# Two heads' attention scores on the two 64-row halves of TensorE, in a float32 model of two transformer blocks

## The chip, the cores and the metric

The program runs on one core of a Trainium2 chip. The metric is the device time of one execution in microseconds, the median of several runs. TensorE multiplies matrices; VectorE (DVE), ScalarE (ACT) and GpSimd (POOL) do the work between; SyncE (SP) issues most of the DMA transfers that bring weights from memory.

## What is computed

Two blocks, one behind the other, on 256 tokens of width 1024, in float32. The first has a retention and a convolution branch and a mixture of 32 experts. The second has two layers; each mixes tokens with four groups of four heads (Fourier, neighbourhood attention, spatial gating, differential attention) and has an MLP. Its first layer is also computed for a context of 256 tokens, whose keys and values the tokens attend to as well. The part of the reference that matters:

```python
def neighbourhood_attention(q, k, v, k_ctx, v_ctx, rpb, rows):
    ...
    s_loc = jnp.einsum('brqhd,brikhd->bhrqik', qg, k_band).astype(jnp.float32) * scale + bias.astype(jnp.float32)
    s_loc = jnp.where(in_win[:, None, :], s_loc, -jnp.inf)
    s_loc = s_loc.reshape(bsz, h, rows, GRID_W, wr * GRID_W)
    s_ctx = jnp.einsum('brqhd,blhd->bhrql', qg, k_ctx).astype(jnp.float32) * scale
    p = jax.nn.softmax(jnp.concatenate([s_loc, s_ctx], axis=-1), axis=-1).astype(v.dtype)
    ...
```

Four heads of width 64, 256 queries; 256 own keys (with bias and window) and 256 keys of the context in the layers. On the context side the same routine runs with the context's own 256 keys, without bias.

## The kernel before

One core does everything in order of stages: the first block, the experts, then the two layers of the second block. The context side of the second block runs beside the experts: `moe` (line 1091) calls `side()` after each expert, which takes the next step of `context_side`. What the context side's matmuls write goes to the two PSUM banks of pool `pf`; the experts use the two of `pm`, and `pa` has four.

In front of the experts stands a branch: `overflow` (line 1157) loads the largest number of tokens that any expert got (`maxcnt`) into a register of every engine and runs a slow path if it is over 32, `with tc.If(rv > 32)` (line 1162). It is not over 32 here, but every engine's instructions in front of the branch stay in front of it.

Weights are float32, in tiles of 1 MB that SyncE loads ahead (`half`, line 243). A matmul with weights goes as three products of tiles split in a high and a low part (`split_w`, line 277). All other matmuls, the scores too, are plain float32; the hardware runs each of them as two passes, and the trace has a record for each pass.

Neighbourhood attention, `na` (line 1366), has eight units per call: two chunks of two heads (c), two halves of the queries (qt), two heads in a chunk (hh). The queries of chunk c lie with head 0 on rows 0 to 63 and head 1 on rows 64 to 127, and so do the keys. A matmul contracts over all 128 rows, so `head_pads` (line 1317) makes two tiles of zeros, and `fill_pad` (line 1326) copies each head's rows out of PSUM into the half that is not to be zero, four copies for two chunks. `two_w` (line 1516) is what the projection calls for that. A unit's first step multiplies such padded queries with the keys of the layer (`own`) and of the context (`kvc`), adds the bias by a matmul (`nab`, with the flipping matrix `k`), takes the softmax (minimum on VectorE, exponential on ScalarE into a tile `e`, or `a` on the context side, then a scaling with the reciprocal sum); its second step, `attend` (line 1348), transposes the probabilities and copies them into `pt`, and after the second head `pv` (line 1355) multiplies them with the values, each head on 64 columns of the array.

The order of the layers' mixer is the string `MIX` (line 26); `mixer` (line 1572) takes a letter at a time: digits are projections, n and d first steps of a unit of neighbourhood and differential attention, b the second step of the oldest open unit, p a part of the output projection (`pj`), and so on. Scores take their PSUM bank from `pm` and `pf` in turn there. On top of that a scheduler, which runs when the program is built, moves instructions of an engine past one another by its own estimate of times. `diff` (line 1451) has the differential attention, with scores `ks`,`qs` over 96 rows.

```python
MIX = "012nndtd3nbbbdndbbbvbndfdbnnsbnpbgdbdxbbbbbp"
```

## Time and profile before

| | |
|---|---|
| runs shown, median (lowest to highest) | 1782.87 us (1780.77 to 1783.07) |
| the profiled execution: its own time | 1776.12 us |
| the profiled execution: span of the trace | 1774.3 us |
| TensorE, matmuls | 1657.3 us busy, 93% of the span |
| TensorE, weight loads | 1317.0 us, 74% |
| VectorE, ScalarE, GpSimd | 54%, 41%, 3% |
| memory read | 486.91 MB |
| granted TensorE clock, mean | 0.982 of 2.4 GHz |

The profile is of one execution, whose own time is the second row; the trace runs from its first to its last instruction. Busy time of TensorE is that of its matmul records, which overlap one another: two passes that start 0.12 us apart each last 0.28 us or more. So rates are read from starts, not from durations. In a timeline a row may stand for several records in a row ("x4"), and its duration is then that from the first start to the last end.

### The profile page before, as it was taken

Reading aid. Unit: us, or ns where it says so; the run is one execution under the profiler, and the core shown is the slowest. Engines: PE = TensorE matmul, PEld = TensorE weight load, DVE = VectorE, ACT = ScalarE, POOL = GpSimd, SP = SyncE. Lnnn points to the kernel's source line nnn. Section 1 sums busy time; section 2 is a strip of 40 time slices with the busy share of each in tenths; the row PEclk is TensorE's granted clock in tenths of the full one; section 3 lists DMA queues with packets and bytes.
Section 4 is the critical chain, followed back from the end, with each engine's and each line's share of the span. In section 5 each row is a group of like instructions: output and inputs, shape, how many; then the busy total and the mean of one; then the engine's idle time right before and its main releaser. Section 6 shows DMA issues by size and latency. Waiting matters only on the chain.

```text
span 1774.3 us, 31435 instructions
## 1 busy us (share of the span) xinstructions
PE 1657.3 (93%) x13088; PEld 1317.0 (74%) x13088; DVE 961.2 (54%) x1719; ACT 724.0 (41%) x1257; POOL 61.6 (3%) x104
## 2 busy tenths in 40 slices
PE   4999999999888998999999997999999999899998
PEld 1678766667565556776677666878999998689998
DVE  5626556467223445544454457586545456766555
ACT  2414434343223433333233336565444445645443
POOL 0000000000000000000000001010000000100000
PEclk9899999999899999999999999999999999989999
DMA  9654588977699999989979997725877746245551
GB/s 372 278 211 169 199 317 310 345 278 265 240 420 420 421 395 407 379 365 420 416 318 401 421 394 268 232 81 172 291 253 264 263 165 208 76 130 188 192 190 43
DMA packets 79060, 495.83 MB, mean 279 GB/s; under 512 B 8928, under 2 KB 15744, under 8 KB 22464
## 3 DMA queue, kind: packets, MB, share of 16 engines
q1 hardware_dynamic: 74496, 478.30, 70.6%
q0 software_dynamic: 3152, 10.47, 2.0%
q10 hardware_dynamic: 1264, 4.98, 0.7%
q8 instruction: 105, 1.72, 0.4%
q14 instruction: 43, 0.35, 0.1%
HBM read 486.91 MB, written 6.82 MB: 278 GB/s over the span
## 4 chain that ended last, share of the span: by engine, by line
PE 64%; DVE 3%; DMA 3%; ACT 2%; issue 2%; POOL 0%; DVEq 0%; ACTq 0%; POOLq 0%
PE pf L200 23%; PE pm L200 19%; PE acc L200 11%; PE pa L200 5%; PE pj L200 3%; PE pm L203 1%; DMA w<-in_w_in 1%; PE pf L203 1%; DMA w<-in_e 1%; PE pada L200 1%; DVE wl L209 1%; DMA w<-in_w_out 1%; DVE sm L1337 1%; ACT e L206 0%; ACT wh L206 0%
## 5 line engine op out<-in xcount | busy, mean ns | idle before, releaser
L209 DVE TENSOR_TENSOR wl<-w,wh 128x1024 fp32r<-128x1024 f32 x346 | 422.4, 1225 | 385.4 <-PE pa L200 100.5
L206 ACT ACTIVATE wh<-w 128x1024 fp32r<-128x1024 f32 x346 | 362.8, 1059 | 407.1 <-PE pa L200 169.5
L200 PE MATMUL pf<-hh,wh 128*128 128x256 f32 x592 | 167.0, 284 | 4.6 <-ACT hh L206 2.4
L200 PE MATMUL pf<-hh,wl 128*128 128x256 f32 x592 | 164.4, 283 | 2.1 <-DVE wl L209 2.1
L200 PE MATMUL pf<-hl,wh 128*128 128x256 f32 x592 | 165.3, 281 | 0.5 <-DVE hl L209 0.5
L200 PE MATMUL acc<-hh,wh 128*128 128x256 f32 x512 | 143.5, 280 | 0.0
L200 PE MATMUL acc<-hl,wh 128*128 128x256 f32 x512 | 142.9, 279 | 0.0
L200 PE MATMUL acc<-hh,wl 128*128 128x256 f32 x512 | 142.9, 279 | 0.0
L200 PE MATMUL pm<-w,xg 128*32 128x256 f32 x2048 | 131.2, 387 | 2.7 <-ACT sm L206 1.8
L200 PEld LDWEIGHTS pf<-hh,wh 128*128 128x128 f32 x592 | 111.8, 189 | 9.8 <-ACT hh L206 3.1
L200 PEld LDWEIGHTS pf<-hh,wl 128*128 128x128 f32 x592 | 110.5, 189 | 5.0 <-DVE wl L209 2.8
L200 PEld LDWEIGHTS pf<-hl,wh 128*128 128x128 f32 x592 | 111.8, 189 | 1.5 <-DVE hl L209 0.9
L200 PEld LDWEIGHTS pm<-w,xg 128*32 128x32 f32 x2048 | 66.6, 111 | 50.9 <-issue 11.2
L200 PEld LDWEIGHTS acc<-hh,wh 128*128 128x128 f32 x512 | 96.4, 188 | 5.9 <-ACT wh L206 4.2
L200 PEld LDWEIGHTS acc<-hh,wl 128*128 128x128 f32 x512 | 96.8, 189 | 0.0
L200 PEld LDWEIGHTS acc<-hl,wh 128*128 128x128 f32 x512 | 96.4, 188 | 0.0
L200 PE MATMUL pada<-w,csil 128*32 128x512 f32 x576 | 83.7, 613 | 5.6 <-DMA w<-in_ada_w 5.6
L200 PE MATMUL pm<-w,ex 128*32 128x256 f32 x1024 | 63.6, 388 | 24.0 <-issue 22.3
L200 PE MATMUL pm<-hh,wh 128*128 128x256 f32 x256 | 71.7, 280 | 0.0
L200 PE MATMUL pm<-hl,wh 128*128 128x256 f32 x256 | 71.7, 280 | 0.0
L200 PE MATMUL pm<-hh,wl 128*128 128x256 f32 x256 | 71.5, 279 | 0.0
L200 PEld LDWEIGHTS pm<-w,ex 128*32 128x32 f32 x1024 | 33.8, 111 | 46.6 <-issue 28.9
(512 smaller groups left out, 3484.7 us busy)
## 6 DMA issues: line engine op xcount, KB each, us to landing
w<-in_e SPq DMA_DIRECT2D x192, 1024.0 KB, 12.1
w<-in_ff SPq DMA_DIRECT2D x96, 1024.0 KB, 5.6
w<-in_ada_w SPq DMA_DIRECT2D x72, 1024.0 KB, 7.1
w<-in_w_in SPq DMA_DIRECT2D x54, 1024.0 KB, 7.8
w<-in_w_out SPq DMA_DIRECT2D x16, 1024.0 KB, 7.0
w<-in_ret_w_o SPq DMA_DIRECT2D x4, 1024.0 KB, 5.2
w<-in_w_su SPq DMA_DIRECT2D x3, 1024.0 KB, 6.5
adab<-in_ada_b SPq DMA_DIRECT2D x9, 256.0 KB, 12.6
```

Of the source, the lines that this page charges most:

```text
L200: return self.nc.tensor.matmul(out, lhsT, rhs, start=start, stop=stop, skip_group_check=True)
L203: return self.nc.tensor.transpose(out, in_, self.ident)
L206: return self.nc.scalar.activation(out, in_, f, **k)
L209: return self.nc.vector.tensor_tensor(out, a, b, op=op)
L1337: self.nc.vector.tensor_reduce(mn, s, AX.X, ALU.min)
```

## The change

`na` no longer takes padded queries but the queries as they come out of the projection, scaled by -0.125 in the one copy out of PSUM (`two_w` with a pair). A new inner function `scores` computes both heads of a chunk for one half of the queries: it takes two PSUM banks, and for each kind of keys multiplies rows 0 to 63 of the queries and keys into the first bank and rows 64 to 127 into the second; then bias and softmax of both. It runs in the first step of head 0; the first step of head 1 does nothing any more. `head_pads` remains for the context's differential attention.

```diff
-    def head_pads(self, w):
+    def head_pads(self):
 
         pads = []
         for c in range(2):
-            t = self.t4([P, 4, 256], F32, "pad") if w == 32 else self.t2([P, 2, 256], F32, "pad")
+            t = self.t4([P, 4, 256], F32, "pad")
...
-    def na(self, pads, ks, vs, bias, put):
+    def na(self, qs, ks, vs, bias, put):
...
         n = 2 * len(ks)
-        pts = {}
+        pts, es = {}, {}
+
+        def scores(c, qt):
+            ps = [self.ps() for _ in range(2)]
+            for (i, k), hh in itertools.product(enumerate(ks), range(2)):
+                r = slice(64 * hh, 64 * hh + 64)
+                self.mm(ps[hh][:, i * 256:(i + 1) * 256], qs[r, c, qt * P:(qt + 1) * P], k[r, c, :], i == 0, True)
+            for hh, p in enumerate(ps):
+                if bias is not None:
+                    self.mm(p[:, :256], self.flip, bias[:, qt, :, 2 * c + hh, :], False, True)
+                sm = self.sm([P, 1])
+                es[c, qt, hh] = e = self.softmax_parts(p[:, :n * P], n * P, sm)
+                self.nc.vector.reciprocal(sm, sm)
+                self.scaled(e, sm, n * P, POOL[0])
 
         def unit(c, qt, hh):
-            h = 2 * c + hh
-            p = self.ps()
-            for i, k in enumerate(ks):
-                self.mm(p[:, i * 256:(i + 1) * 256], pads[c][:, hh, qt * P:(qt + 1) * P], k[:, c, :], i == 0, True)
-            if bias is not None:
-                self.mm(p[:, :256], self.flip, bias[:, qt, :, h, :], False, True)
-            sm = self.sm([P, 1])
-            e = self.softmax_parts(p[:, :n * P], n * P, sm)
-            self.nc.vector.reciprocal(sm, sm)
-            self.scaled(e, sm, n * P, POOL[0])
+            if hh == 0:
+                scores(c, qt)
             yield
             if hh == 0:
                 pts[c, qt] = self.t4([P, 2, 4, P], F32, "pt")
-            self.attend(e, pts[c, qt][:, hh], n)
+            self.attend(es[c, qt, hh], pts[c, qt][:, hh], n)
...
+            elif isinstance(d, tuple):
+                self.act(d[0], p, scale=d[1])
...
-        npad = self.head_pads(64)
-        self.lin(self.chunk(W[0]), 8, 512, [WJob(lhs, self.two_w(npad, nk))])
+        nq = new("nq")
+        self.lin(self.chunk(W[0]), 8, 512, [WJob(lhs, self.two_w((nq, -0.125), nk))])
...
-        na = self.na(npad, [nk, kvc[0]], [nv, kvc[1]], bias, put)
+        na = self.na(nq, [nk, kvc[0]], [nv, kvc[1]], bias, put)
```

`mixer` makes and fills `nq` in the same way.

The order of TensorE's instructions moves with it. First the branch in front of the experts, before (`wh`, `wl`, `hh`, `hl` are the context's value projection, `cnt` counts tokens):

```order
L200 MATMUL pf_3409<-wh_3458,hh_2818 128x512
L200 MATMUL pf_3409<-wl_3459,hh_2818 128x512
L200 MATMUL pf_3409<-wh_3458,hl_2819 128x512
L200 MATMUL pf_4030<-kvc_2793,pad_3277 128x256
L1161 TENSOR_LOAD maxcnt
L1162 COMPARE_AND_BRANCH
```

One score of the context stands in front of the branch, nothing else of its attention. Now:

```order
L200 MATMUL pm_3240<-cnt,router 128x32 x2
L200 MATMUL pm_3240<-cnt,sm_3238 128x32 x3
L200 MATMUL pf_4024<-kvc_2793,nq_3277 128x256
L200 MATMUL pf_4025<-kvc_2793,nq_3277 128x256
L203 MATMUL pf_4043<-ident_81,a_741_4029 128x128 x2
L203 MATMUL pf_4047<-ident_81,a_744_4036 128x128 x2
L200 MATMUL pf_4051<-pt_4042,kvc_2793 64x128
L1161 TENSOR_LOAD maxcnt
L1162 COMPARE_AND_BRANCH
```

Two scores, four transposes of two heads' probabilities and one product with the values stand in front of it, and the five count matmuls, which stood ten matmuls ahead of the projection's end, stand behind the projection.

Second, the first scores of the first layer's mixer, before (`pf` and `pm` are the two banks):

```order
L200 MATMUL pf_10831<-own_10458,pad_10465 128x256
L200 MATMUL pf_10831<-kvc_10398,pad_10465 128x256
L200 MATMUL pf_10831<-nab_10459,k_1942_10395 128x256
L200 MATMUL pm_10842<-own_10458,pad_10465 128x256
L200 MATMUL pm_10842<-kvc_10398,pad_10465 128x256
L200 MATMUL pm_10842<-nab_10459,k_1942_10395 128x256
```

Head 0 and its bias, then head 1 and its bias. Now:

```order
L200 MATMUL pf_10819<-own_10452,nq_10459 128x256
L200 MATMUL pm_10820<-own_10452,nq_10459 128x256
L200 MATMUL pf_10819<-kvc_10392,nq_10459 128x256
L200 MATMUL pm_10820<-kvc_10392,nq_10459 128x256
L200 MATMUL pf_10819<-nab_10453,k_1941_10389 128x256
L200 MATMUL pm_10820<-nab_10453,k_1941_10389 128x256
```

The two heads alternate, and the two biases follow. The second layer's first scores stand alike; the second scores of the first layer stand head by head, four in a row, with both biases behind.

Third, the first layer's third scores, before (head 0 alone; head 1 follows 39 rows later):

```order
L203 MATMUL pf_11153<-ident_81,e_11062 128x128 x4
L200 MATMUL pf_11170<-own_10458,pad_10467 128x256
L200 MATMUL pf_11170<-kvc_10398,pad_10467 128x256
L200 MATMUL pf_11170<-nab_10459,k_1942_10395 128x256
L203 MATMUL pm_11115<-ident_81,e_11040 128x128 x4
```

All of these are 128 rows on 128 columns. Now:

```order
L203 MATMUL pm_11103<-ident_81,e_11039 128x128 x4
L200 MATMUL pf_11158<-own_10452,nq_10459 128x256
L200 MATMUL pf_11158<-kvc_10392,nq_10459 128x256
L200 MATMUL pf_11158<-nab_10453,k_1941_10389 128x256
L200 MATMUL pm_11147<-pt_11095,own_10452 64x128 x4
L200 MATMUL pm_11147<-pt_11095,kvc_10392 64x128 x4
L200 MATMUL pf_11180<-ks_10735,qs_10734 128x512
L200 MATMUL pm_11159<-own_10452,nq_10459 128x256
L200 MATMUL pm_11159<-kvc_10392,nq_10459 128x256
L200 MATMUL pm_11159<-nab_10453,k_1941_10389 128x256
L200 MATMUL pm_11188<-ks_10735,qs_10734 128x512
```

The two heads stand apart, each between matmuls of other shapes. The fourth scores and those of the second layer from the second on are apart as well; in the fourth, eight products with the values stand even between a head's own keys and the context's.

## Rows read from the trace of the kernel before

**Rows 1.** Busy time by stage: stretch, us, engines' busy us (records), granted clock, DMA share, GB/s.

```profile
545.00:1075.00 530.00, 488.19 (x4744) 350.56 (x4738) 260.24 (x476) 177.10 (x348) 15.81 (x33) 0.99 0.97 396
...
1088.00:1235.00 147.00, 136.56 (x945) 117.99 (x944) 100.06 (x223) 83.24 (x161) 17.18 (x21) 0.98 0.53 160
1441.00:1590.00 149.00, 137.23 (x933) 118.48 (x932) 101.62 (x217) 85.59 (x165) 11.99 (x14) 0.95 0.43 137
```

The engines are PE, PEld, DVE, ACT, POOL.

**Rows 2.** The same view around the branch.

```profile
440.00:450.00 10.00, 8.56 (x42) 6.53 (x40) 4.16 (x21) 2.30 (x8) 0.00 (x0) 1.00 0.54 199
450.00:460.00 10.00, 4.84 (x23) 4.87 (x24) 1.00 (x5) 0.46 (x1) 0.50 (x1) 0.52 0.15 58
```

**Rows 3.** Timeline of PE, first scores: start us, us, engine, line, operation, out<-in, rows*columns, count.

```profile
1132.96 0.59 PE L200 MATMUL pf<-own,pad 128*128 128x256 f32 x2
1133.39 0.59 PE L200 MATMUL pf<-kvc,pad 128*128 128x256 f32 x2
```

**Rows 4.** Timeline of PE in the expert stage: matmuls of 32 columns, and of 32 rows.

```profile
463.38 3.98 PE L200 MATMUL pm<-w,xg 128*32 128x256 f32 x64 [0.61 <-ACT sm L206]
...
494.93 0.29 PE L200 MATMUL acc<-yh,sc 32*128 32x256 f32 x4
495.05 0.28 PE L200 MATMUL acc<-yl,sc 32*128 32x256 f32 x4
```

**Rows 5.** Timeline of PE at changes of shape, in the mixer and in the expert stage.

```profile
1156.62 0.28 PE L200 MATMUL pa<-hh,wl 128*128 128x256 f32 x1
1156.83 0.43 PE L200 MATMUL pm<-pt,own 128*64 128x128 f32 x2
1157.19 0.39 PE L200 MATMUL pa<-hh,wh 128*128 128x256 f32 x1
1157.42 0.28 PE L200 MATMUL pa<-hl,wh 128*128 128x256 f32 x1
1157.54 0.28 PE L200 MATMUL pa<-hh,wl 128*128 128x256 f32 x1
...
490.48 0.70 PE L200 MATMUL pf<-kvc,pad 128*128 128x256 f32 x2
491.11 1.07 PE L200 MATMUL pm<-w,ex 128*32 128x256 f32 x16
```

**Rows 6.** The line of the branch: engine, operation, count, ns min/median/max, first and last start.

```profile
L1162 PEldq COMPARE_BRANCH  x1: 5329/5329/5329, 449.1 to 449.1; - x1
```

**Rows 7.** Timeline of all engines around the branch.

```profile
447.99 0.67 PE L200 MATMUL pf<-kvc,pad 128*128 128x256 f32 x2
...
448.70 0.42 DVE L1337 TENSOR_REDUCE sm<-pf 128x1 f32<-128x256 f32 x1 [0.82 <-PE pf L200]
...
449.16 0.47 ACT L206 ACTIVATE a<-pf,sm 128x256 f32<-128x256 f32 x1 [0.57 <-DVE sm L1337]
449.53 0.19 ACT L206 ACTIVATION_READ_ACCUMULATOR a<-pf,sm 128x1 f32 x1
454.66 0.49 DVE L209 TENSOR_TENSOR oh<-router,pos 128x128 f32<-128x128 f32 x2 [5.41 <-PEq L1162]
455.07 0.16 DVE L1381 RECIPROCAL sm<-sm 128x1 f32<-128x1 f32 x1
...
455.26 0.35 DVE L218 TENSOR_SCALAR a<-a,sm 128x256 f32<-128x256 f32 x1
...
461.95 0.37 ACT L206 ACTIVATE pt<-pf 128x256 f32<-128x256 f32 x1
```

**Rows 8.** Timelines of ACT and PE: the context's queries and keys out of PSUM.

```profile
433.71 1.55 ACT L206 ACTIVATE pad<-pf 64x256 f32<-64x256 f32 x4 [1.56 <-PE pf L200]
435.29 0.60 ACT L206 ACTIVATE kvc<-pf 128x512 f32<-128x512 f32 x1
...
435.31 0.50 PE L200 MATMUL pf<-wh,hh 128*128 128x512 f32 x1 [1.00 <-ACT pad L206]
```

**Rows 9.** Timeline of PE, last third of the first mixer: a wait.

```profile
1187.08 0.66 PE L203 MATMUL pm<-ident,e 128*128 128x128 f32 x4 [1.20 <-ACT pt L206]
```

More of the change, by code (lines that the diff above doesn't have):

```diff
@@ L1554, in context_mixer @@
         yield
-        yield from itertools.islice(self.in_turn(self.na(npad, [nk], [nv], None, put), 0), 1, None, 2)
-        dpad = self.head_pads(32)
+        yield from itertools.islice(self.in_turn(self.na(nq, [nk], [nv], None, put), 0), 1, None, 2)
+        dpad = self.head_pads()
         self.lin(self.chunk(W[1]), 8, 512, [WJob(lhs, self.two_w(dpad, dk))])
@@ L1581, in mixer @@
         bias = self.na_bias(l, held)
-        npad = self.head_pads(64)
+        nq = new("nq")
         dq, fa, sv, su = (None,) * 4
-        na = self.na(npad, [nk, kvc[0]], [nv, kvc[1]], bias, put)
+        na = self.na(nq, [nk, kvc[0]], [nv, kvc[1]], bias, put)
         qk_d = [self.tc.dram_tile([P, 1024], F32, name=f"{n}_d{l}") for n in ("q", "k")]
@@ L1589, in mixer @@
             if step == "0":
-                self.lin(w or self.chunk(W[0]), 8, 512, [WJob(lhs, self.two_w(npad, nk))])
+                self.lin(w or self.chunk(W[0]), 8, 512, [WJob(lhs, self.two_w((nq, -0.125), nk))])
             elif step == "t":
```

## The prediction

> **What bounds the kernel now.** I read the busy time by stage first. The expert stage waits for weights: from 545 to 1075 us the DMA engines are busy 0.97 of the time. The two attention mixers, each with what adjoins it, wait for TensorE: 136.56 of 147 us and 137.23 of 149 us, at half the DMA load [rows 1]. So a microsecond of TensorE counts in the mixers and is covered in the expert stage. Between the two lies a hole: from 450 to 460 us the DMA engines are at 0.15 and TensorE is busy for half the time [rows 2]. That is the branch on the largest expert load, which every engine passes. Weights are prefetched until all buffers are full, and none comes free before TensorE works on the first expert. Whatever moves that moment moves the whole expert stage, which then again runs at the speed of its weights.
>
> The timeline around the branch shows who opens it: TensorE's own compare-and-branch takes 5.33 us [rows 6], VectorE waits 5.41 us for it, and the first one-hot tile is made only behind it [rows 7]. TensorE reaches that branch at 449.1 [rows 6], 1.1 us after its last matmul before it began (447.99, the only score matmul that stands there now) [rows 7]. VectorE and ScalarE have no more than 0.6 us of work left then, and 5 us to do it in.
>
> **The change, part by part.** All counts are of hardware passes: one fp32 matmul is two of them, 0.43 us for 256 columns [rows 3], so 0.215 us each.
>
> (1) Work in front of the branch. Before, one score stood there. Now there are both scores, four transposes, and the first product with the values, which waits for two softmaxes. The queries come out of PSUM in one copy, 0.60 us like that of the keys, instead of four in 1.55 us, and the value projection waited 1.00 us for these [rows 8]. So it starts about 0.9 us earlier, and the scores at 447.1 instead of 447.99; that the ten count matmuls now stand behind the whole projection changes the sum of TensorE's work ahead of the scores by nothing. From there, by the durations of [rows 7]: scores 0.7 (447.8); minimum of the first head 0.42, its exponential and accumulator 0.57 from start to end (448.9 with the hops); the second head's exponential and accumulator stand behind that on ScalarE, with one short activation between, 0.8 (449.8 to 449.9); reciprocal 0.16 and scaling 0.35, with one other operation between them (450.45); two transposing passes 0.4, no longer than two of a score [rows 3] (450.85); copy 0.37 (451.25); then the product may start. The branch follows 1.1 us behind it: 452.4 instead of 449.1. **+3.3 us**, all of it on the path. Bounds: -0.9 us if TensorE's sequencer runs past the waiting matmul, so that only the earlier start remains; +4.3 us if each of the ten hops costs 0.1 us more. I take +3.3: in the rows of both other engines the branch work begins after the last waiting instruction had started, never ahead of it.
>
> (2) The array in the layers. A visit is one pair of heads for one half of the queries: eight scores' passes over keys of two kinds, four visits in each of two layers. Four 32-row matmuls side by side show what overlap can give: they start together and the next four follow 0.12 us later [rows 4]. Two halves in one slot save 4 x 0.215 = 0.86 us a visit. But the order decides, not the source: the two heads alternate in the first visit of each layer alone; in the first layer's second visit they stand behind one another without a gap; in the other five, 128-row bias matmuls, products with the values or latent scores stand between the heads, and there is nothing to overlap with. So three visits save: **-2.6 us**. Bounds: 0 (no overlap at all) and 8 x 0.86 = -6.9 us.
>
> In that, passes of the second head overtake those of the first. The row for it: 64 passes on four column strips in 3.98 us, 0.06 us each, more than three at a time although each matmul's two passes use the same strip [rows 4]. The Trainium skill, "TensorE: Matmul & The Clock Gate" (The mechanism), has it that matmuls start strictly in program order. By that page the alternating visits would take five slots and the adjoining one seven, -1.5 us in place of -2.6 and 1788.7 in place of 1787.6; the row speaks against it.
>
> (3) Switches between shapes of the array. Before, a score is a 128-row matmul among 128-row matmuls and costs no switch. Now each goes over to 64 rows and back. The trace has no 64-row matmul; nearest are the 64-column ones. In a stream of full-width passes 0.12 us apart, the first pass of another shape starts 0.21 us behind the last, and on the way back the pass behind the first starts 0.23 us after it: 0.09 and 0.11 us over the rate, 0.2 us a switch. A score between two such shapes took 490.48 to 491.11 = 0.63 us where 0.43 is its rate: 0.2 us again [rows 5, 3]. I count, from the order, 12 more switches in the first layer (2, 2, 4, 4 by visit) and 14 in the second (2, 4, 4, 4). 26 x 0.2 = **+5.2 us**. Bounds: 26 x 0.09, the first gap alone, +2.3 us, and +5.2 us; I take 0.2, which both rows give.
>
> The Trainium skill, "TensorEngine Tiling (Array Packing)" (Key Properties), speaks against this change in the same place: changing the tiling mode, not just the tile, drains the engine. The trace agrees with 0.2 us a switch; without that rule the sum would be 5.2 us less, -0.5 us. The page gives no price.
>
> (4) The context side in the expert stage has four such visits of two matmuls each. Their gain (0.43 us a visit) and their switches lie beside weight loads at 0.97 [rows 1]: 0. If that cover went, they would be -1.7 us and some +2 us.
>
> (5) ScalarE's four query copies become one in each layer, 0.9 us less [rows 8], and the GpSimd clearing goes. Both lie beside the next projection, which writes other PSUM banks: 0. If that cover were gone, -1.8 us.
>
> (6) Softmax work of the second head moves up. In the last third of each mixer TensorE waits for the attention chain, once 1.20 us for a copy of the transposed probabilities [rows 9]; now one score group less stands there, and the output projection's matmuls fill in. I take one such wait gained per two layers, **-1.2 us**; bounds -2.4 us (one in each) and +2.4 us, since two PSUM tiles are claimed at once, which may make latent scores wait as long.
>
> Sum: 3.3 - 2.6 + 5.2 - 1.2 = +4.7 us. The profiled execution took 1776.12 us (span 1774.3 and 1.8 around it), so 1780.8; the median of the runs shown is 1782.87, 6.75 us above it, and with the same difference the forecast is **1787.6 us**. A measurement of this kernel tells changes over about 0.2% (3.6 us) from none, so 1779.3 and 1786.4 part the three outcomes.
>
> **The rivals.** (A) The branch is not delayed: TensorE's sequencer goes past the product that waits for the softmax, and the 5.33 us run beside it. For it: the branch needs the count, not the attention. Against it: the starts in [rows 7]. Then (1) is -0.9 and the sum +0.5: 1783.4, no change. (B) Faster: the mixers' idle TensorE is taken up. It is 10.4 and 11.8 us around the two [rows 1]; if earlier softmaxes let the output projection fill half of that, 11 us go instead of 1.2: 3.3 - 2.6 + 5.2 - 11 = -5.1, 1777.8. It decides from 9.5 us recovered (5.9 and the 3.6 that can be told). For it: fillers stand between the late attention steps in the new order. Against it: much of that idle time is normalisation and lies outside attention. (C) The packing does nothing: passes of the two halves run one behind the other, and only the switches stay. Then +7.3, 1790.2. For it: no 64-row pair stands in this trace; against it, [rows 4]. (D) The halves overlap in all eight visits, because TensorE pulls the second head's passes across the 128-row matmuls between: 3.3 - 6.9 + 5.2 - 1.2 = +0.4, 1783.3. The order speaks against it, and no row shows a pass that overtakes one of another shape. The Trainium skill, "TensorEngine Tiling (Array Packing)" (Theoretical Speedup), gives up to twice the rate for 64 rows, which is this rival.
>
> **How the numbers follow.** Forecast 0.40, A 0.22, B 0.18, C 0.15, D 0.05. The forecast's own spread by its bounds leaves a fifth of it below 1786.4 and the rest above, so slower is 0.32 + 0.15 and a little of A, 0.48; same is 0.08 with most of A, D and some of B, 0.33; faster what is left of B and a little of A, 0.19. The range runs from 1779 (short of B) to 1794 (C with both waits of part 6 turned to a loss, 7.3 + 3.6 = 10.9).
>
> **What would show it.** TensorE's compare-and-branch at 452 to 453 us and the hole in the DMA longer by 3 us would show (1), at 448 to 449 would show A. Score matmuls with 64 rows: in the first visit pairs that start within 0.02 us show the overlap, in the third and fourth single passes 0.215 us apart; a start gap of 0.2 us at each change of shape shows (3). I am wrong if the branch opens no later and the mixers are not longer, and most if the mixers lose several microseconds of TensorE's idle time.

## The result and the profile after

The changed kernel takes 1793.34 us (median of 4 runs, 1791.66 to 1795.37), the kernel before beside it 1781.82 us (1780.67 to 1783.07): a ratio of 1.0079, 95% interval 1.0061 to 1.0098. It is slower by 11.5 us where +4.7 us had been forecast. The profiled execution of the changed kernel took 1791.66 us, with a span of 1789.9 us.

The branch, TensorE's row for its line as in [rows 6]:

```profile
L1162 PEldq COMPARE_BRANCH  x1: 3412/3412/3412, 451.9 to 451.9; - x1
```

It starts 2.8 us later and ends 0.9 us later than before, since it takes 3.41 us in place of 5.33. TensorE's timeline around it, in the columns of [rows 3]:

```profile
447.37 0.70 PE L200 MATMUL pf<-kvc,nq 64*128 64x256 f32 x4
449.86 0.96 PE L203 MATMUL pf<-ident,a 128*128 128x128 f32 x4 [1.78 <-DVE sm L992]
450.74 0.43 PE L200 MATMUL pf<-pt,kvc 128*64 128x128 f32 x2
455.44 0.87 PE L200 MATMUL pf<-pt,kvc 128*64 128x128 f32 x5 [4.26 <-PEq L1162]
458.38 0.37 PE L200 MATMUL pf<-pt,kvc 128*64 128x128 f32 x1 [2.07 <-issue]
458.68 1.22 PE L200 MATMUL pf<-kvc,nq 64*128 64x256 f32 x2
459.83 5.11 PE L200 MATMUL pm<-oh,xn 128*128 128x128 f32 x32
...
468.24 3.66 PE L200 MATMUL pm<-w,xg 128*32 128x256 f32 x64
```

Behind the branch six more passes of products with the values come first, with a stop of 2.07 us among them, and a score, before TensorE gathers the first experts' tokens at 459.83 (before at 455.16). The first expert's matmuls begin at 468.24, 4.9 us later than in [rows 4].

The scores. First the first visit of the first layer, then its second visit, then head 0 of the third:

```profile
1141.04 0.39 PE L200 MATMUL pa<-wh,hl 128*128 128x512 f32 x1
1141.36 0.48 PE L200 MATMUL pf<-own,nq 64*128 64x256 f32 x1
1141.36 0.48 PE L200 MATMUL pm<-own,nq 64*128 64x256 f32 x1
1141.67 0.38 PE L200 MATMUL pf<-own,nq 64*128 64x256 f32 x1
1141.68 0.38 PE L200 MATMUL pm<-own,nq 64*128 64x256 f32 x1
...
1142.11 0.38 PE L200 MATMUL pf<-kvc,nq 64*128 64x256 f32 x1
...
1142.42 0.70 PE L200 MATMUL pf<-nab,k 128*128 128x256 f32 x2
1142.95 0.59 PE L200 MATMUL pm<-nab,k 128*128 128x256 f32 x2
...
1159.28 0.48 PE L200 MATMUL pf<-own,nq 64*128 64x256 f32 x1
1159.30 0.48 PE L200 MATMUL pm<-own,nq 64*128 64x256 f32 x1
...
1159.82 0.38 PE L200 MATMUL pf<-kvc,nq 64*128 64x256 f32 x1
...
1173.83 0.70 PE L200 MATMUL pf<-own,nq 64*128 64x256 f32 x2
1174.36 0.59 PE L200 MATMUL pf<-kvc,nq 64*128 64x256 f32 x2
1174.88 0.70 PE L200 MATMUL pf<-nab,k 128*128 128x256 f32 x2
```

The two heads start together: eight passes take four slots of 0.215 us, and each change of shape costs a little: the first pass of the new shape starts about 0.1 us late (0.32 us behind the 512 columns of 1141.04, whose like follow one another every 0.23 us), and the second 0.32 us after it (1141.36 to 1141.67) where the rate is 0.215, so 0.2 us a change. On balance such a visit gains 0.86 - 0.4 = 0.46 us. In the second visit head 1's first pass (1159.30) starts ahead of head 0's passes on the context's keys (1159.82), which stand before it in the program. In the third visit nothing overlaps: own keys 0.53 us and the context's 0.52, where 0.43 each is the rate of [rows 3].

What the forecast did not have is in the last third of the mixers:

```profile
1195.24 0.60 PE L203 MATMUL pf<-ident,e 128*128 128x128 f32 x4
1197.03 1.14 PE L200 MATMUL pf<-sguw,sv 128*64 128x128 f32 x16 [1.20 <-ACT pt L206]
1198.61 0.50 PE L200 MATMUL pf<-ks,qs 96*128 96x512 f32 x1 [0.43 <-ACT e L206]
1200.74 0.69 PE L203 MATMUL pm<-ident,rb 128*128 128x128 f32 x2 [1.63 <-DVE rb L1502]
1201.36 1.22 PE L200 MATMUL pm<-own,nq 64*128 64x256 f32 x2
1202.38 1.06 PE L200 MATMUL pm<-kvc,nq 64*128 64x256 f32 x2
1203.37 1.22 PE L200 MATMUL pm<-nab,k 128*128 128x256 f32 x2
```

TensorE waits 1.20, 0.43 and 1.63 us within five microseconds. Before, this stretch had waits of 1.20 [rows 9], 0.69 and 0.17 us, and two scores behind them:

```profile
1188.42 0.50 PE L200 MATMUL pm<-ks,qs 96*128 96x512 f32 x1 [0.69 <-ACT pt L206]
1189.10 0.66 PE L203 MATMUL pm<-ident,e 128*128 128x128 f32 x4 [0.17 <-ACT e L206]
```

In the changed kernel every matmul behind the waits takes about twice its time (own keys 1.02 us from start to start, 0.53 in the third visit): TensorE has gone from 2.4 to 1.2 GHz. Two windows, columns as in [rows 1]: ten microseconds around this place with a granted clock of 0.67, and the whole first mixer with 0.94 where it had 0.98.

```profile
1200.00:1210.00 10.00, 9.26 (x45) 7.53 (x45) 3.98 (x8) 2.41 (x6) 1.57 (x2) 0.67 0.18 64
...
1088.00:1235.00 147.00, 134.71 (x894) 113.02 (x893) 99.24 (x216) 82.20 (x166) 16.19 (x18) 0.94 0.51 156
```

**Where the time went**, by starts of the same matmuls in all traces that the study made: the first and the last pass of the experts' first product (`pm<-w,xg`), the first `pa<-hl,wh` of the layers, and each mixer from its first score to the MLP's first `pm<-hh,wh`. All in us; the kernels are those of the next section.

| trace | first expert | last expert | layers begin | mixer 1 | mixer 2 | span |
|---|---|---|---|---|---|---|
| before, two executions | 463.4, 462.7 | 1068.3, 1069.2 | 1096.5, 1096.9 | 101.0, 103.8 | 99.9, 99.8 | 1774.3, 1776.3 |
| changed, two executions | 468.2, 468.6 | 1074.8, 1074.9 | 1104.4, 1105.4 | 104.7, 104.6 | 102.0, 102.0 | 1789.9, 1791.6 |
| layers_only | 464.5 | 1070.9 | 1099.8 | 104.8 | 102.0 | 1786.0 |
| context_only | 470.0 | 1076.0 | 1106.4 | 103.5 | 99.3 | 1786.8 |
| joint_padded | 465.2 | 1076.4 | 1105.0 | 105.2 | 99.9 | 1789.8 |
| single_rows | 469.0 | 1080.9 | 1110.0 | 108.2 | 104.5 | 1800.0 |
| before_side1 | 458.8 | 1075.2 | 1110.5 | 102.2 | 100.0 | 1787.5 |
| after_side1 | 458.7 | 1076.6 | 1110.0 | 105.9 | 103.0 | 1794.9 |
| late_padded | 462.9 | 1070.6 | 1098.3 | 103.0 | 100.5 | 1778.1 |
| two_visits | 465.0 | 1074.5 | 1102.2 | 103.5 | 97.8 | 1781.4 |
| late_rows | 462.9 | 1071.6 | 1099.3 | 108.5 | 100.1 | 1785.8 |
| chain_behind | 464.6 | 1074.0 | 1104.0 | 103.8 | 102.3 | 1789.3 |
| two_visits_tied | 464.0 | 1070.8 | 1098.5 | 103.4 | 100.0 | 1778.4 |

Two places hold the loss: the layers begin about 6 us later (seven traces with the old context side: mean 1098.8; changed twice, context_only and chain_behind: 1105.0), and the mixers are 2.1 and 2.5 us longer (before twice, context_only and before_side1: means 102.6 and 99.8; changed twice, layers_only, after_side1 and chain_behind: 104.8 and 102.3). Together that is 11 us, near the 11.5 of the medians. The rest of the layers is left out: the stretches behind each mixer come out in two lengths some 1.7 us apart from trace to trace, in the kernel before too.

Single traces of the first column have to be read with care. In the seven with the old context side TensorE, VectorE and ScalarE have the very same order of instructions from the first expert to the layers, and still the layers begin anywhere from 1096.5 to 1102.2. Nor is a late start taken up there: two_visits has the latest first expert of the seven, 1.6 us behind before, and the latest layers, 5.8 us behind. The changed kernel twice and context_only share one order too, and again the later start has the later layers: 468.2, 468.6 and 470.0 go with 1104.4, 1105.4 and 1106.4.

### The profile page after: what moved, and what is told of

It reads as the page before. It is cut to its first block, busy times and chain, and to the rows that moved or that the text cites. A ratio compares the mean times of both kernels' runs of the same rounds, so it can differ in the third digit from the quotient of the medians.

```text
span 1789.9 us, 31419 instructions
## 1 busy us (share of the span) xinstructions
PE 1671.1 (93%) x13088; PEld 1318.6 (74%) x13088; DVE 965.2 (54%) x1719; ACT 718.8 (40%) x1248; POOL 58.8 (3%) x98
## 5 line engine op out<-in xcount | busy, mean ns | idle before, releaser
L209 DVE TENSOR_TENSOR wl<-w,wh 128x1024 fp32r<-128x1024 f32 x346 | 423.0, 1226 | 384.7 <-PE pa L200 96.2
```

The costliest lines, as they stand in the source:

```text
L209: return self.nc.vector.tensor_tensor(out, a, b, op=op)
```

## The experiments

The first theory, O, was that the loss follows from the order: the branch's delay in the expert stage, and later stalls in the mixers. Its rivals are named with each run.

**layers_only and context_only**: the change in one place alone, with the old `na` kept as `na_old` in the other. For layers_only:

```diff
 def context_mixer(...)
-        nq = new("nq")
+        npad = self.head_pads(64)
...
-        yield from itertools.islice(self.in_turn(self.na(nq, [nk], [nv], None, put), 0), 1, None, 2)
+        yield from itertools.islice(self.in_turn(self.na_old(npad, [nk], [nv], None, put), 0), 1, None, 2)
```

> The two layers as changed, the context side in the expert stage as before (padded queries, one head per step). Theory O (order): the loss has two places, the branch (attention work in front of it and the value products right behind it, first expert 4.9 us later) and the mixers (+3.8 and +2.7 us, from later stalls of TensorE in which its clock falls). Then the branch is back at 449 us, the first expert matmul at 463 to 464 us, and the mixers keep their loss: 1782 + 6.5 = 1788 to 1789 us. Rival X (expert stage): the branch's delay is covered by the weights, since at 880 us of the changed run it had gone to -0.4 us; then this kernel is as slow as the whole change, 1792 to 1794 us. Rival M: the mixers' loss is a chance of one profile; then 1782 to 1784 us.

> The context side as changed, the layers as before. Theory O: 1782 + 4.9 = 1786 to 1788 us, with the first expert matmul at 468 us and both mixers as long as before. Rival X: 1782 to 1783 us although the first expert is late.

layers_only: 1786.91 us, ratio 1.0042 (1.0026 to 1.0057), +7.5 us. context_only: 1787.43 us, ratio 1.0050 (1.0031 to 1.0069), +8.9 us. Both halves lose, and within their intervals they add up to the whole. The first expert comes at 464.5 and 470.0, where theory O had 463 to 464 and 468. The times of rivals X and M did not come. X's premise, that a late start can be made up within the stage, comes back below, with the windows of the changed kernel.

**joint_padded and single_rows**: the order without the array form, and the array form without the order.

```diff
 def scores(c, qt):
-                r = slice(64 * hh, 64 * hh + 64)
-                self.mm(ps[hh][:, i * 256:(i + 1) * 256], qs[r, c, qt * P:(qt + 1) * P], k[r, c, :], i == 0, True)
+                self.mm(ps[hh][:, i * 256:(i + 1) * 256], qs[c][:, hh, qt * P:(qt + 1) * P], k[:, c, :], i == 0, True)
```

```diff
 def unit(c, qt, hh):
+            r = slice(64 * hh, 64 * hh + 64)
...
-                self.mm(p[:, i * 256:(i + 1) * 256], pads[c][:, hh, qt * P:(qt + 1) * P], k[:, c, :], i == 0, True)
+                self.mm(p[:, i * 256:(i + 1) * 256], qs[r, c, qt * P:(qt + 1) * P], k[r, c, :], i == 0, True)
```

> Both heads' scores in one step as in the change, but with the padded 128-row queries of before: the order of the change in the layers without its array halves and without changes of shape; in front of the branch two scores and no transposes. Theory O: the stalls belong to the order, so the mixers lose about as much as in the changed kernel, less 0.2 us for each change of shape and plus 0.5 us for each of three overlapping visits that are gone: +4 to +6 us, 1786 to 1788 us. Rival A (array): the cost is the 64-row shape and its changes; then the mixers are as long as before and the time is 1782 to 1784 us.

> 64-row queries without zeros, but one head per step in the order of before: nothing overlaps, and each of 16 score groups in the layers changes shape twice. Theory O with 0.2 us a change: 32 x 0.2 = +6.4 us in the mixers, and about +2 us at the branch, in front of which one softmax's transposes now stand: 1789 to 1791 us, with the stalls where they were before. Rival A: more than that, over 1793 us, since the shape costs more than its changes. Rival M (changes of shape hide behind other waits): 1784 us.

joint_padded: 1791.29 us, ratio 1.0070 (1.0048 to 1.0092); single_rows: 1797.93 us, 1.0101 (1.0080 to 1.0122). joint_padded lies above what any theory had, and single_rows above O and where rival A had it, over 1793. The table says why: the layers begin at 1105 and 1110, though joint_padded's first expert is only 2 us late. The scheduler has put much of the expert stage in another order. The mixers alone, against the means above: joint_padded loses 2.6 us in the first and 0.1 in the second, single_rows, where every 64-row score stands alone, 5.6 and 4.7, which is more than 32 changes of shape (6.4 us). So A holds for the mixers in part, and what stands over goes with the clock: from 45 to 75 us behind each mixer's first score, where the waits are, the low clock takes 5.1 and 6.8 us from single_rows and 0 and 1.7 from before.

**after_side1 and before_side1**: one step of the side generator in place of two in front of the branch.

```diff
-SIDE, SIDE0 = 1.0, 2
+SIDE, SIDE0 = 1.0, 1
```

> The changed kernel with one side step in place of two in front of the branch: no score, transpose or product with values stands there. Theory B (the delay at the branch is on the path): TensorE reaches its compare-and-branch at 448 us or earlier, the first expert matmul starts near 462 us, the hole in the DMA is 5 us shorter, and the time falls by 4 to 6 us against the changed kernel, to 1787 to 1789 us. Theory P (place in the order): the expert stage reaches its end by the order in which side work and experts stand behind one another, which every change of the context's steps deals anew; then the first expert comes early and the end of the expert stage gains nothing, 1792 to 1796 us.

> The control to it: the kernel before with one side step in place of two in front of the branch, nothing else. Theory B: first expert about 1 us earlier, the same time within 2 us. Theory P: the order of the expert stage is dealt anew, and the time changes by 4 us or more although nothing of the attention has changed; the end of the expert stage moves by as much.

after_side1: 1798.83 us, ratio 1.0112 (1.0090 to 1.0134), above the forecasts of both theories. before_side1: 1794.49 us, 1.0085 (1.0062 to 1.0109). In the second nothing of the attention has changed. Its first expert begins 4 to 5 us earlier than before, and its layers begin 14 us later (12 against the mean of the seven). So an early first expert bought nothing in these two, and an edit that only deals the expert stage anew costs as much as the whole change. B falls for this edit, P stands in the control. What it doesn't tell is whether the later end comes from the order or from the step that was moved behind the branch.

**chain_behind** goes on from there: the changed kernel, steps as they are, with the first context visit's transposes and products held until the gather is issued.

```diff
 def unit(c, qt, hh):
             if hh == 0:
+                while held:
+                    rest(*held.pop(0), self.gmark)
                 scores(c, qt)
             yield
+            if bias is None and (c, qt) == (0, 0):
+                held.append((c, qt, hh))
+            else:
+                rest(c, qt, hh)
```

`rest` is the second step of a unit as it was; `self.gmark` is the gather's last matmul, and the first transpose is ordered behind it.

> The changed kernel with one edit in the expert stage: the transposes and products with values of the context's first visit are held until the gather of the first experts has been issued, so that in front of the branch only the two scores stand and nothing of the attention between the branch and the gather. Theory B (this chain is the delay): compare-and-branch at about 449.5 us in place of 451.9, first expert matmul at 464 to 465 us in place of 468.2 to 468.6, the stretch from the first to the last expert matmul at 606 us as it was, and 3 to 4 us off the time: 1789 to 1790 us, ratio 1.006. Theory P (newly dealt order): the first expert comes early and the stretch behind it gets longer by as much, 1792 to 1794 us, as in joint_padded (first expert at 465.2, stretch 611.2).

1792.08 us, ratio 1.0081 (1.0063 to 1.0098): no faster than the change. The edit did what it was to do; its branch and TensorE's timeline:

```profile
L1162 PEldq COMPARE_BRANCH  x1: 3852/3852/3852, 449.5 to 449.5; - x1
```

```profile
447.54 0.70 PE L200 MATMUL pf<-kvc,nq 64*128 64x256 f32 x4
454.02 0.98 PE L200 MATMUL pm<-oh,xn 128*128 128x128 f32 x3 [5.78 <-DVE oh L209]
456.48 5.80 PE L200 MATMUL pm<-oh,xn 128*128 128x128 f32 x29 [1.49 <-issue]
...
464.58 3.66 PE L200 MATMUL pm<-w,xg 128*32 128x256 f32 x64
```

The gather starts 5.8 us earlier than in the changed kernel and the first expert 3.7 us earlier, but the last expert comes at 1074.0 (1074.8 and 1074.9 in the changed kernel) and the layers begin at 1104.0. The earlier start did not bring the end forward here, and where the time was lost can be read off. From 607.3 to 914.2 us TensorE runs the very instructions of the kernel before, 2686 matmul records on end, and is never more than 1 us behind it. Then the orders part, and the last expert comes 5.7 us later than before, the layers 7.5. So in this kernel the loss belongs to the order behind 914 us and not to the start. The windows show the same; the last two columns are DMA share and GB/s. Before:

```profile
890.00:940.00 50.00, 47.83 (x432) 39.57 (x434) 25.34 (x35) 15.83 (x27) 0.40 (x1) 1.00 0.79 311
...
985.00:1045.00 60.00, 54.14 (x530) 39.12 (x528) 29.20 (x41) 20.45 (x33) 1.21 (x3) 1.00 0.99 409
```

The changed kernel:

```profile
890.00:940.00 50.00, 48.41 (x445) 38.57 (x444) 23.70 (x34) 16.06 (x27) 0.80 (x2) 1.00 0.90 368
...
985.00:1045.00 60.00, 53.72 (x545) 39.90 (x545) 27.02 (x39) 18.62 (x34) 1.20 (x3) 1.00 0.92 374
```

chain_behind:

```profile
890.00:940.00 50.00, 48.41 (x434) 40.38 (x433) 25.79 (x35) 16.50 (x27) 0.40 (x1) 1.00 0.81 323
...
985.00:1045.00 60.00, 53.76 (x543) 40.35 (x543) 26.89 (x38) 18.20 (x33) 1.21 (x3) 1.00 0.93 375
```

From 890 to 940 us the DMA is idle a fifth of the time before. The changed kernel moves 368 GB/s there in place of 311, 2.9 MB more, which is 6.8 us at the 421 GB/s of the stretch from 940 to 985 us. There it is level with before although it started 4.9 us late: the 24th expert's first product begins at 901.25 before and at 900.81 in the changed kernel. A late start alone does not use the idle time up: two_visits, in the order of before, is 5.0 us late there (906.27), moves 318 GB/s and keeps its delay. chain_behind, which starts almost as early as before, moves 323. From 985 to 1045 us it is the other way: the transfers are busy 0.92 and 0.93 of the time in the new orders in place of 0.99, whatever came before (before_again 0.99, layers_only 0.98; joint_padded 0.91). That is 0.06 x 60 = 4 us, of the size of the 3 to 6 us by which the last expert of these kernels is behind the mean of the seven, 1070.8. That buffers come free later there would explain it; it is not shown which ones.

For the changed kernel itself this leaves the cause of the 6 us in part open. In its own order it gains 6.8 us in the one window and loses 35 x 60 / 421 = 5 us in the other, and at the end it is late by about as much as at the start. No kernel has its late order with an early start, so the runs don't tell how much of the 6 us is the late start and how much the order.

A last piece stands behind the last expert. Before, then the changed kernel:

```profile
1073.74 0.39 PE L200 MATMUL acc<-yh,sc 32*128 32x256 f32 x4 [1.11 <-ACT yh L206]
...
1074.55 0.28 PE L200 MATMUL acc<-yl,sc 32*128 32x256 f32 x4
1074.76 0.74 PE L200 MATMUL pf<-wh,hch 128*128 128x512 f32 x2
```

```profile
1080.72 0.39 PE L200 MATMUL acc<-yh,sc 32*128 32x256 f32 x4 [0.52 <-ACT yh L206]
1081.35 0.50 PE L200 MATMUL pf<-wl,hch 128*128 128x512 f32 x1 [0.23 <-DVE wl L209]
...
1084.67 0.29 PE L200 MATMUL acc<-yl,sc 32*128 32x256 f32 x4
```

Twelve matmuls of the context's last projection have got between the accumulating matmuls, 4.0 us from the first to the last in place of 0.8; some 2 of these 3 us more come back before the layers begin (from the last expert to the layers 28.2 us before, 29.5 now).

**late_padded** keeps the joint order of layers_only and gives the last two visits of each layer their 128 rows back; **late_rows** keeps the order of before and gives these visits 64 rows. In both, the context side is the old one, and the queries are the padded ones, of which the 64-row scores read one half.

```diff
 def scores(c, qt):
-                r = slice(64 * hh, 64 * hh + 64)
-                self.mm(ps[hh][:, i * 256:(i + 1) * 256], qs[r, c, qt * P:(qt + 1) * P], k[r, c, :], i == 0, True)
+                r = slice(64 * hh, 64 * hh + 64) if c == 0 else slice(0, P)
+                self.mm(ps[hh][:, i * 256:(i + 1) * 256], qs[c][r, hh, qt * P:(qt + 1) * P], k[r, c, :], i == 0, True)
```

```diff
 def unit(c, qt, hh):
+            r = slice(64 * hh, 64 * hh + 64) if c else slice(0, P)
...
-                self.mm(p[:, i * 256:(i + 1) * 256], pads[c][:, hh, qt * P:(qt + 1) * P], k[:, c, :], i == 0, True)
+                self.mm(p[:, i * 256:(i + 1) * 256], pads[c][r, hh, qt * P:(qt + 1) * P], k[r, c, :], i == 0, True)
```

> Layers alone, context as before: the joint order of the change, with 64-row halves (rows of the padded queries) in the first two visits of each layer, where they overlap, and 128-row scores in the last two. Against layers_only this differs in the array form of the last two visits and in the copies of the queries alone. Theory C (clock): in that kernel the mixers lose because 64-row scores stand in the stretch in which TensorE has just waited, and the low clock lasts twice as long there (3.4 us lost in each mixer, 1.7 with 128-row scores in the same order); then 3.4 us of clock and 2 x 8 changes of shape of 0.2 us come back: 1780 to 1783 us, ratio near 1.001. Theory O (order alone): as layers_only, ratio 1.003 to 1.005.

> The kernel before, in its own order, with one edit: in the last two visits of each layer each head's score reads the 64 rows of the queries and keys that are not zero. Nothing overlaps; the array does half of what it did there, and each score group changes shape twice (16 groups' changes in all, 8 groups with 2 each: 16 x 0.2 = 3.2 us). Theory C: 64-row scores beside the waits of the mixers' last third lengthen the low clock; the mixers lose 3 to 5 us of clock each in place of 1.7, and the time is 1784 to 1788 us (ratio 1.003 to 1.004). Theory S (changes of shape alone): +3.2 us or less, no more clock lost than before, 1782 to 1783 us (ratio 1.001 to 1.002). Rival N: nothing, as with the padded queries, within 1 us of before.

late_padded: 1778.79 us, ratio 0.9995 (0.9982 to 1.0007), below what both theories had; O's 1.003 to 1.005 falls. late_rows: 1781.27 us, 1.0005 (0.9987 to 1.0023), where N and S can't be told apart and C's 1784 to 1788 did not come. With layers_only's 1.0042 that is a square with one bad corner: neither the joint order nor the late 64-row scores cost anything that can be measured, the two together cost 7 us. The square is not quite exact: late_rows has the order of before in both mixers, but in late_padded 64 of 673 rows of TensorE in the first mixer and 23 of 625 in the second stand elsewhere than in layers_only. The windows of layers_only and of late_padded, each from 1190 and from 1540 us on (last columns: granted clock, DMA share, GB/s):

```profile
1190.00:1200.00 10.00, 6.74 (x41) 4.69 (x39) 7.54 (x20) 4.01 (x7) 1.33 (x1) 0.79 0.34 107
1200.00:1210.00 10.00, 10.00 (x75) 9.35 (x76) 5.13 (x9) 5.32 (x10) 1.04 (x1) 0.87 0.24 67
...
1550.00:1560.00 10.00, 9.06 (x43) 7.72 (x44) 3.65 (x7) 2.63 (x6) 1.78 (x2) 0.66 0.11 44
```

```profile
1190.00:1200.00 10.00, 7.53 (x48) 6.45 (x49) 6.21 (x18) 3.44 (x8) 2.09 (x2) 0.83 0.34 107
1200.00:1210.00 10.00, 10.00 (x88) 9.04 (x88) 6.95 (x13) 6.23 (x13) 0.28 (x1) 1.00 0.62 198
1540.00:1550.00 10.00, 6.74 (x43) 5.48 (x42) 7.38 (x19) 4.45 (x9) 1.40 (x1) 0.83 0.32 105
```

The waits of the joint order are in both (1.19 or 1.20, 0.43 and 1.63 or 1.64 us). But in late_padded the low clock takes (1 - 0.83) x 10 = 1.7 us from each mixer there; in layers_only it takes 2.1 + 1.3 = 3.4 us from the first and 3.4 us from the second. The same 3.4 us stand in both profiles of the changed kernel, and in after_side1 and chain_behind too, while joint_padded, in a joint order with 128 rows, has 1.7 us there in each mixer. Before has none there in the first and 1.7 in the second, in both profiles. What the edit moves in the mixers by the table, 1.8 + 1.5 = 3.3 us, is of the size of this clock or of the 16 changes of shape that went with the rows (16 x 0.2 = 3.2 us); with the clock low the two can't be told apart. Over all their runs (12 each), the mean span falls from 1784.8 to 1777.7 us, and the time that the clock takes, span times (1 - mean clock), from 45.7 to 38.8 us. So theory C has the better of O for the joint order. It does not carry over to the order of before: the clock takes 8.5 us from the first mixer in late_rows' profile, whose execution took 1787.57 us, and nothing from the last third of its second, and its median is that of before all the same. How long the clock stays low after such a wait, from run to run, stays open.

**two_visits and two_visits_tied**: what looked good in the change, put together. Both heads together in the first two visits of each layer, one head per step with 128 rows in the others, context as before; in the second kernel the biases are ordered behind the last score, so that all four early visits should overlap.

```diff
 def unit(c, qt, hh):
-            if hh == 0:
-                scores(c, qt)
+            if c:
+                scores(c, qt, (hh,))
+            elif hh == 0:
+                scores(c, qt)
```

```diff
 def scores(c, qt, hs=None):
...
-                    self.mm(p[:, :256], self.flip, bias[:, qt, :, 2 * c + hh, :], False, True)
+                    b = self.mm(p[:, :256], self.flip, bias[:, qt, :, 2 * c + hh, :], False, True)
+                    if len(ps) > 1:
+                        self.behind(b, last)
```

> Layers alone, context as before: both heads together on the two halves in the first two visits of each layer, which lie among projections; the last two visits one head per step with padded queries, as before. What the runs so far leave as good of the change: four overlapping visits, each 0.86 us less work and 0.4 us of shape changes. Theory C or O: 4 x 0.46 = -1.8 us, 1777 to 1779 us beside 1779 to 1780 of before, no clock lost in addition. Rival: whatever moves a softmax earlier empties a later stretch; then the mixers are 2 us longer, 1781 to 1783 us.

> two_visits with the bias matmul of the first head tied behind the second head's last score, so that in the second layer's second visit too the two halves stand side by side. Four overlapping visits in place of three: one more time 0.86 us less work and two changes of shape fewer (0.4 us): 1.3 us below two_visits, 1776 to 1778 us, ratio 0.998. Rival: the first head's softmax starts 0.9 us later for the tie, and the time is that of two_visits or of before, ratio 0.999 to 1.000.

1779.21 us, ratio 0.9986 (0.9972 to 1.0001), and 1780.10 us, ratio 1.0007 (0.9993 to 1.0021). The harm is gone. But the tie did not do what it was for: in two_visits_tied's second layer the two heads of the second visit still stand apart, head 0's scores from 1505.94 us and head 1's from 1507.43, now with two matmuls of a projection between them in place of the bias. So three visits overlap in both kernels, a fourth was not tried, and the passes show a gain of 3 x 0.46 = 1.4 us less some 0.8 us of changes of shape in the visit that stands apart. That is within what a measurement can't tell from nothing. No version of the study is measurably faster than the kernel before.

**before_again and after_again**: second profiles.

> The kernel before once more, for a second profile of it: how far its mixers, its expert stage and its clock differ between two executions of one program. If the clock lost in the mixers is 0 to 2 us in the first and under 6 in the second again, the 3.1 and 6.1 us of the changed kernel are more than chance; if it is 3 in the first here too, they are not.

> The changed kernel once more, for a second profile of it. Expected: the first expert 4 to 5 us late again and the last expert 6 to 8 us late, since both follow from the order; 3 us of clock lost in the first mixer and 6 in the second, if the clock follows from the 64-row scores.

1778.07 and 1793.38 us, one run each. The changed kernel's mixers repeat to 0.1 us. The first mixer of before does not: 101.0 and 103.8, since in the second execution the clock falls once behind the attention, at 1226 us. Its second mixer repeats. So the changed kernel's loss in the second mixer repeats, and that in the first is 1 to 4 us. The expectation had it that 3 us of clock lost in the first mixer of before too would make the changed kernel's 3 us there no more than chance, and 3.4 were lost; what sets the changed kernel apart is that it loses them in the attention each time.

## Why the prediction was right or wrong

The sign, the likeliest of the three outcomes and the range were right. The size was not: +4.7 us against +11.5. Two steps failed, by about 3 us each: the expert stage, where (1) and (4) together had +3.3 and the layers begin 6 us late, and (6) in the mixers, which had -1.2 and came to about +2.

**(1) Work in front of the branch, +3.3 us.** The chain of hops came out nearly as worked out: the branch starts at 451.9, the forecast was 452.4. That its end follows by the same 3 us failed: the branch took 3.41 us in place of 5.33. What then delayed the first expert by 4.9 us was the rest of the products, a score and a stop behind the branch, which the working did not have. The sentence "Whatever moves that moment moves the whole expert stage" holds only while the order stays: within one order a later first expert goes with later layers on the whole, but across orders first experts from 458.7 to 470.0 us end in last experts from 1074.0 to 1076.6 us in all kernels with a new order but single_rows. I read 0.97 of the DMA's time as a stage that runs at the speed of its weights throughout; 3% of 530 us are 16 us, and most of them stand in one window, 890 to 940 us.

**(4) The context side in the expert stage, 0.** This is where the working of the stage failed. I had the cover of its own work (weight loads) and looked at the changed instructions alone; but the scheduler moved hundreds of others. Of TensorE's 5702 matmul records between the first expert and the layers some 3600 are left in the sequence of before. What a new order costs by itself the runs show twice: the control, in which one step of the context side moves and nothing of the attention changes, has its layers 14 us later, and chain_behind loses 5.7 us behind the place where its order leaves that of before. How much of the changed kernel's 6 us is order and how much the late start of (1) stays open.

**(2) Overlap in three visits, -2.6 us.** Held, pair for pair, and only in these three: the first and second visit of the first layer and the first of the second. In the first layer's second visit the program has all passes of one head ahead of the other's, and they start in pairs, 0.02 us apart, so the second head's do overtake (1159.30 ahead of 1159.82). The Trainium skill, "TensorE: Matmul & The Clock Gate" (The mechanism), lets matmuls start in program order alone; this row speaks against it for passes on different rows of the array.

**(3) Changes of shape, +5.2 us.** The price of 0.2 us each held: 0.1 us at the first pass and 0.1 at the second, into 64 rows and out of them. The Trainium skill's rule that a change of tiling mode drains the engine, "TensorEngine Tiling (Array Packing)" (Key Properties), agrees with it, and the page has no price.

**(5) Copies and clearing, 0.** Nothing in the traces speaks against it; it was not tried alone.

**(6) Waits of the mixers, -1.2 us.** Wrong, and with it the sum of the mixers: (2), (3) and (6) make +1.4 us, measured are +4.6, so that with (2) and (3) as they held (6) is about +2.0. One wait was indeed shortened, but the remaining ones moved together, the scores that stood between them had been done early, and TensorE came out of them at 1.2 GHz, with 64-row scores to do: in the last third of the mixers the clock takes 3.4 us each in place of 0 and 1.7. The clock was in [rows 1], 0.98 and 0.95 for the two mixers, and I had not asked what my own term does to it.

**The rivals.** C gave 1790.2 us, the nearest time, by a mechanism that the first visit refutes. A and B did not come, D neither: no pass crossed a 128-row matmul.

## What to carry to other kernels

Where a scheduler deals the order of a long stage, an edit to one small part is an edit to the whole stage: change a number that has nothing to do with it, as a control, and see what a new order costs by itself before pricing the edit. A transfer share just below one doesn't mean that every stretch runs at the speed of its transfers: find the places where the queue waits, since an order can gain or lose several microseconds there. Compare starts within one order before saying that a stage takes up a late start. And packing gains where the two halves stand side by side among work that doesn't wait, here 0.46 us a visit, which no kernel turned into a time that could be measured. Next to waits, half-array matmuls went with a longer low clock in the joint order.

## What the runs showed of the hardware

TensorE's compare-and-branch takes 5.2 to 5.3 us in the seven traces with the old context side and the old number of steps, 3.3 to 3.6 us in the changed kernel and context_only, 3.8 in single_rows, 3.9 in chain_behind, 4.2 in joint_padded, 4.5 in before_side1 and 5.4 in after_side1. Where it is short, a stop with nothing that the profile shows to wait for follows a few matmuls later: 3.41 and then 2.07 us, 3.59 and 2.40, 3.77 and 1.74, 3.85 and 1.49, 4.19 and 1.92, 4.45 and 0.56. The sums are from 5.0 to 6.1 us, so the branch costs about as much everywhere, now or a little later. What is being waited for the profile doesn't show. On VectorE, ScalarE, GpSimd and SyncE the same branch takes 45 to 72 ns in the traces of before and of the change.

Passes of float32 matmuls on the two 64-row halves of the array start 6 to 13 ns apart, in the second visit of the first layer against their order in the program. A 128-row matmul between the halves ends this: none of the five visits with other matmuls between the heads has such a pair.
